# Branch B's output product by blocks of two with seven products, its operands and weight sums formed through HBM, and branch A's gate kept in HBM

## The chip, the cores and the metric

The kernel runs on one core of one Trainium2 chip. The metric is the device time of one execution in microseconds (us), the median of several runs. Names of engines: PE is TensorE (matmuls), DVE VectorE, ACT ScalarE, POOL GpSimd, SP SyncE, whose queue issues most DMAs.

## The reference

Two layers over 1024 latent tokens of width 1024. Layer 0 has two branches behind one input projection and one output projection; layer 1 is a pooling mixer and isn't touched by the change. Cut to layer 0:

```python
def layernorm(x, g, b):
    mu = jnp.mean(xf, axis=-1, keepdims=True)
    var = jnp.mean(jnp.square(xf - mu), axis=-1, keepdims=True)
    y = (xf - mu) * lax.rsqrt(var + LN_EPS) * g + b

def conformer_conv(va, vg, p):
    u = va * jax.nn.sigmoid(vg)
    u = depthwise_conv(u, p["conv_w"], p["conv_b"], CONV_PAD)     # 31 taps
    return jax.nn.silu(layernorm(u, p["ln_g"], p["ln_b"]))

def even_mixer(h, h0, p):
    z = h @ p["w_in"]
    va, vg, ga, xb, gb = jnp.split(z, [W_CONV, 2 * W_CONV, 3 * W_CONV, 3 * W_CONV + W_LRU], axis=-1)
    y_a = conformer_conv(va, vg, p) * jax.nn.silu(ga)
    y_b, hT = rglru_branch(xb, p, h0, True)      # short conv, gates, a scan in each direction
    y_b = y_b * jax.nn.silu(gb)
    return jnp.concatenate([y_a, y_b], axis=-1) @ p["w_out"], hT

# per layer: x = x + gate * even_mixer(modulate(rmsnorm(x), shift, scale)); shift, scale, gate = silu(c) @ mod_w + mod_b
```

## The kernel before

Activations stand transposed: eight tiles of 128 channels (rows) by 1024 tokens (columns), in two halves of 512 tokens, since one matmul writes 128 x 512. Every product is in three parts: an operand x is split into a rounded high part (a cast on ACT) and the rest (a subtraction, "low"), and hi·hi, hi·lo and lo·hi are added up in PSUM. A weight tile of 128 x 1024 comes as `wr` (raw, a ring of two buffers), is cast on ACT to `wh` and its low part `wl` formed on POOL (`raw_split`). A product over eight input tiles and both halves is 48 matmuls.

In the first layer the engines' orders are written out by hand: each call through `on(engine, ...)`, and its short forms `vec`, `act`, `cast` and `gp`, is tied behind the call before on that engine. So one late instruction holds all that stand behind it there. `fill(n)` puts n pieces of the depthwise convolution (DVE) between other work. The stages in order:

1. A loop over the eight channel tiles j: the products `va`, `vg`, `xb`, the recurrent branch's gates and its two scans on DVE. `rec_sum` adds the two directions (DVE, 128 x 1024) and SP stores the sum to `yb_raw[j]` in HBM. `at_rest` and the next block's weight loads follow.
2. The gate products `gb` of branch B with their SiLU (`gb_product`, `gb_silu`); `gated(n)` reloads `yb_raw[n]` through a ring of two buffers (`vtile`), multiplies and splits (ACT cast, POOL low).
3. The product with branch B's half of the output weights, `wob` (from the loop `for m in range(KT)` behind `wob_ps`): for each output tile m and half 24 matmuls, then `wob_evict`: ACT scales with the layer's gate into one of four buffers (`ttile`), SP loads x into a `vtile`, POOL adds, SP stores to `x1_part` in HBM. Under this product the rest of the convolution is done, and near its end the layer norm: `ln_mean`, then for each half `ln_square` and `ln_add` (DVE and ACT), `mean_parts` (cast `mh_ln` on ACT, low `ml_ln` on DVE), and `ms_ln`, two matmuls with a matrix of ones that sum over channels. `ln_root` (root on ACT, reciprocal on DVE), `ln_scale` (eight multiplications on DVE a half) and `ln_silu` (eight on ACT) follow.
4. The gate products `ga` of branch A (two of them in the fixed order), their SiLU and `ga_evict`, a multiplication on DVE out of PSUM. From here on (`fixed[0] = False`) a scheduler orders the work. Then branch A's half of the output product, `woa`, already by blocks of two with seven products (`quad`): with inputs and weights cut into 2 x 2 blocks, seven products of sums of blocks (`b11, t1, t2, b21, t3, b22, t4`) take the place of eight.
5. The second layer's modulation vector: `mod_halves` loads tiles of 128 x 512 into `ttile` buffers and multiplies them on DVE with the condition vector `cH`, with a running sum.

The gate's multiplications, means and tiles named here are the ones that the change moves.

Of the kernel before, what the change touches and what calls it, by code (L numbers as in the profile page):

```python
# [49 lines left out]

@with_exitstack
def body(ctx, tc, xT, ctxT, cc, ccol, modT, modW, win, gw, wout, wu, grp, wg, wo1, small, edge, ident, outT):
# [15 lines left out]
    y_raw = [{n: dram.tile([P, 2 * S], F32, tag=f"y_{n}_{p}", name=f"y_{n}_{p}") for n in BOPS} for p in range(2)]  # L68
    x1_part = [dram.tile([P, S], F32, tag=f"x1_part{j}", name=f"x1_part{j}") for j in range(KT)]
# [168 lines left out]
    a0 = base.tile([P, 2, KT], F32, name="a0")  # L238
    m1 = base.tile([P, 1, 3 * KT], F32, name="m1")
# [456 lines left out]
    def raw_load(src, name):  # L696
        raw = wpool.tile([P, D], F32, tag="wr", name=f"wr_{name}")
        nc.sync.dma_start(raw, src)
        return raw

# [76 lines left out]
    NSPREAD = 5  # L777

# [41 lines left out]
    with ExitStack() as actx:  # L820
# [56 lines left out]
        def rec_sum(st):  # L877
            hs, hb = st[2][1], st[2][3]
            vec(nc.vector.tensor_tensor, out=hs[:, C:], in0=hs[:, C:], in1=hb[:, C:], op=add)
            nc.sync.dma_start(yb_raw[st[0]], hs[:, C:])  # L880
# [22 lines left out]
        for j in range(KT):  # L903
# [73 lines left out]
            name = "gb1" if final else f"vg{j + 1}"  # L977
            raw = raw_load(win[4 * KT + 1] if final else win[KT + j + 1], name)
# [9 lines left out]
            if state is not None:  # L988
                for d in range(2):
                    rec_scan(state, d)  # L990
                rec_sum(state)
            at_rest()
            xb = wide(name if final else f"xb{j + 1}")
# [16 lines left out]
            fill(19 if state is None else 6)  # L1010
            state, uc = now, ucn


        gps = {0: [xb[:, h] for h in HALF]}
        gws = {}


        def gb_weights(j):
            src, name = ((win[4 * KT + j], f"gb{j}") if j < KT else
                         (wout[j - KT, 1], f"wob{j - KT}") if j < 2 * KT else  # L1020
                         (win[2 * KT + (0, KT // 2)[j - 2 * KT]], f"ga{(0, KT // 2)[j - 2 * KT]}"))
            gws[j] = raw_split(raw_load(src, name), name)

        def gb_product(j, w):
            if j == 4:
                gps[j] = (lambda t: [t[:, h] for h in HALF])(wide(f"gb{j}"))
            else:
                gps[j] = [psum(f"gb{j}_{h}") for h in range(2)]
            for h in range(2):
                all_of(mm3_fixed(gps[j][h], w, (hh, hl), HALF[h]))  # L1030
# [3 lines left out]
        def gb_silu(j):  # L1034
            sbs[j] = [ttile(f"sb{j}_{h}") for h in range(2)]
            for h in range(2):
                act(sbs[j][h], gps[j][h], AF.Silu)

        gb_product(1, w)
# [3 lines left out]
        gb_weights(2)  # L1043
        rec_exp(state)
        gb_product(2, gws[2])
# [3 lines left out]
        gb_weights(3)  # L1049
        gb_silu(0)  # L1050
        gb_silu(1)
        gb_product(3, gws[3])
        fill(24)
        rec_scan(state, 0)
        raw = raw_load(win[4 * KT + 4], "gb4")
        hi = wpool.tile([P, D], F32R, tag="wh", name="wh_gb4")
        lo = wpool.tile([P, D], F32R, tag="wl", name="wl_gb4")
# [4 lines left out]
        rec_sum(state)  # L1062
# [18 lines left out]

    KH = KT // 2
# [66 lines left out]
    def prod(ps, w, op, first, last):  # L1149
        xh, xl = op  # L1150
        for k in range(KH):
            hi, lo = w[:, k * P : (k + 1) * P], w[:, H + k * P : H + (k + 1) * P]
# [65 lines left out]
    bh, bl = [], []  # L1218
    def gated(n, between):
        th, tl = d2tile(f"ybh{n}", F32R), d2tile(f"ybl{n}", F32R)  # L1220
        for h in range(2):
            y = vtile(f"yr{n}_{h}")
            nc.sync.dma_start(y, yb_raw[n][:, HALF[h]])
            v = sbs[n][h]
            vec(nc.vector.tensor_tensor, out=v, in0=y, in1=v, op=mult)
            cast(th[:, HALF[h]], v)
            gp(out=tl[:, HALF[h]], in0=v, in1=th[:, HALF[h]].bitcast(F32), op=sub)
            fill(between)
        bh.append(th)
        bl.append(tl)  # L1230

    gb_product(4, gws[4])
    gated(0, 3)
    gb_silu(2)
    gb_weights(5)
    gb_product(5, gws[5])
    gated(1, 3)
    for j in range(3, KT + 1):
        if j == 4:
            gb_weights(j + 2)  # L1240
        if j < KT:
            gb_silu(j)
        if 4 < j < KT - 1:
            gb_weights(j + 2)
        if 3 < j < KT - 2:
            gb_product(j + 2, gws[j + 2])
        gated(j - 1, (0, 0, 4, 5, 5, 3, 1, 0)[j - 1])
        if j == KT:
            gb_weights(KT + 1)
            fill(8)  # L1250
        ln_sums()


    def wob_evict(m, h):
        v = ttile(f"wo_{m}_{h}")
        act(v, wob_ps[m][h], AF.Identity, scale=m0[:, 0, 2 * KT + m : 2 * KT + m + 1])
        t = vtile(f"xp{m}_{h}")
        nc.sync.dma_start(t, xT[m][:, HALF[h]])
        gp(out=t, in0=t, in1=v, op=add)
        nc.sync.dma_start(x1_part[m][:, HALF[h]], t)  # L1260


# [50 lines left out]
    wob_ps = {}  # L1313
    for m in range(KT):
        w = gws[KT + m]
        wob_ps[m] = [psum(f"wob{m}_{h}") for h in range(2)]
        steps = [mm3_fixed(wob_ps[m][h], w, (bh, bl), HALF[h]) for h in range(2)]
        if m == 0:
            for h in range(2):
                for _ in range(KT - 1):  # L1320
                    next(steps[h])
        for h in range(2):
            all_of(steps[h])
            if (m, h) == (KT - 2, 0):
                while ended[0] < KT:
                    fill(1)
                ln_sums()
                for q, parts in enumerate([mean_parts(lnacc[q][:, :H], f"mu{q}") for q in range(2)]):
                    ln_mean(q, parts)
            elif m >= KT - 2:  # L1330
                q = m - KT + 2
                for j in range(KT) if (m, h) != (KT - 1, 1) else ():
                    ln_square(j, q)
                    if j > 1:
                        ln_add(j - 2, q)
                if (m, h) != (KT - 1, 1):
                    for j in (KT - 2, KT - 1):
                        ln_add(j, q)
                    lnparts = mean_parts(lnacc[0][:, :H], "ln0") if q == 0 else lnparts
                else:  # L1340
                    ln_root(0, lnparts)
                    lnparts = mean_parts(lnacc[1][:, :H], "ln1")
            wob_evict(m, h)
            fill(7)
            ln_sums()
        gb_weights(KT + m + 2)


    gaps = {}

    def ga_product(j, w, h):
# [982 lines left out]
```

## Time and profile before

| | |
|---|---|
| runs: median of 3 (lowest to highest) | 1268.27 us (1267.44 to 1268.94) |
| the profiled execution: its span | 1263.6 us, 16209 instructions |
| busy in the span | PE 99%, DVE 90%, ACT 52%, POOL 23% |
| bytes moved | 182.29 MB, 144 GB/s in the mean |
| TensorE clock granted | full speed in all 40 slices |

A span is the time from the first to the last instruction that the profiler recorded; the profiled execution has no time of its own beside it, and the runs lie 4.7 us above that span. Busy times of matmuls overlap each other, so a stretch of matmuls is priced by the distance of their starts. In rows of a timeline the first number is the start in us, the second the time; a bracket says how long the engine idled before and what ended that. A row of a window has start and end, length, each engine's busy time with its count of instructions, the clock, the share of the DMA engines and GB/s.

### The profile page before, as it was taken

The page shows a single profiled execution, that of the slowest core. Times are in us where ns is not written, and L with a number is a line of the kernel's source. Part 1 is how long each engine was busy: PE and PEld are TensorE (multiplying, and loading weights), DVE is VectorE, ACT ScalarE, POOL GpSimd, SP SyncE. Part 2 cuts the span into 40 slices and gives each one's busy share as a digit, 9 for nine tenths or more (in the row PEclk, how much of TensorE's full clock was granted, in tenths as well). Part 3 has the DMA queues.
Part 4 walks back from the last instruction along what each step waited for, and adds up shares of the span by engine and source line. Part 5 has one row for each costly group of instructions (what it writes and reads, how often), then busy time and mean ns, then how long its engine had stood idle before and what let it go on. Part 6 is the DMA issues. An engine that isn't in the chain of part 4 may idle for free.

```text
span 1263.6 us, 16209 instructions
## 1 busy us (share of the span) xinstructions
PE 1249.8 (99%) x5866; PEld 1035.6 (82%) x5866; DVE 1139.3 (90%) x1746; ACT 653.8 (52%) x952; POOL 295.7 (23%) x176
## 2 busy tenths in 40 slices
PE   9999999999999999999999999999999999999997
PEld 7788888888888888888887878888888888888786
DVE  7799999999999999998978969999899987977975
ACT  8464566656666534237535445744343444644642
POOL 0015364436444547543210023000000000000002
PEclk9999999999999999999999999999999999999999
DMA  9970121112121233442436666344323334759723
GB/s 376 388 254 33 52 65 46 63 43 75 42 84 42 84 119 132 159 150 84 147 112 225 202 206 183 103 136 148 125 94 140 117 125 126 268 199 335 285 71 134
DMA packets 78705, 182.29 MB, mean 144 GB/s; under 512 B 7712, under 2 KB 23328, under 8 KB 78624
## 3 DMA queue, kind: packets, MB, share of 16 engines
q1 hardware_dynamic: 67328, 172.33, 39.8%
q10 hardware_dynamic: 11296, 8.92, 2.2%
q8 instruction: 46, 0.75, 0.2%
q14 instruction: 35, 0.29, 0.1%
HBM read 137.18 MB, written 44.04 MB: 143 GB/s over the span
## 4 chain that ended last, share of the span: by engine, by line
PE 70%; DVE 18%; DMA 7%; issue 2%; ACT 2%; POOL 1%; SPq 0%; POOLq 0%; ACTq 0%; DVEq 0%
PE wob L670 7%; DVE conv L670 5%; PE va L670 5%; PE xb L670 4%; PE vg L670 4%; DVE l L670 3%; PE fold L670 3%; PE g L670 3%; PE qb_v L1153 2%; PE ga L670 2%; PE qb_g L1156 2%; PE ga L161 2%; PE qb_v L1156 2%; PE qb_g L1155 2%; PE qb_g L1153 2%
## 5 line engine op out<-in xcount | busy, mean ns | idle before, releaser
L670 DVE SCALAR_TENSOR_TENSOR conv<-u,sm,conv 128x505 f32<-128x505 f32 (+6 forms) x224 | 153.6, 744 | 1.0
L2045 POOL TENSOR_TENSOR o<-x,rr 128x256 f32<-128x256 f32 (+1 forms) x10 | 9.2, 952 | 448.4 <-ACT rr L2045 448.4
L670 ACT ACTIVATE l<-g,sm 128x512 f32<-128x512 f32 (+1 forms) x96 | 58.7, 619 | 57.7 <-PE g L670 57.0
L670 POOL TENSOR_TENSOR l<-l,l 128x1280 f32<-128x1280 f32 x16 | 47.1, 2967 | 25.6 <-ACT l L670 15.1
L670 PE MATMUL gb<-h0h,wl_gb 128*128 128x512 f32 x128 | 49.9, 390 | 0.4 <-POOL wl_gb L670 0.4
L670 PE MATMUL va<-h0h,wl_va 128*128 128x512 f32 x128 | 49.9, 390 | 0.2 <-DVE wl_va L670 0.2
L98 ACT CAST wq_g<-wr_g 128x512 fp32r<-128x512 f32 x48 | 28.2, 621 | 41.9 <-DMA wr_g<-wg 15.6
L670 PE MATMUL gb<-h0l,wh_gb 128*128 128x512 f32 x128 | 49.8, 389 | 0.0
L670 PE MATMUL gb<-h0h,wh_gb 128*128 128x512 f32 x128 | 49.8, 389 | 0.0
L670 PE MATMUL va<-h0l,wh_va 128*128 128x512 f32 x128 | 49.8, 389 | 0.0
L670 PE MATMUL va<-h0h,wh_va 128*128 128x512 f32 x128 | 49.8, 389 | 0.0
L670 PE MATMUL wob<-ybl,wh_wob 128*128 128x512 f32 x128 | 49.8, 389 | 0.0
L670 PE MATMUL wob<-ybh,wl_wob 128*128 128x512 f32 x128 | 49.8, 389 | 0.0
L670 PE MATMUL wob<-ybh,wh_wob 128*128 128x512 f32 x128 | 49.8, 389 | 0.0
L670 DVE TENSOR_TENSOR_SCAN l<-l,l 128x256 f32<-128x256 f32 (+1 forms) x32 | 48.7, 1521 | 1.1
L670 DVE SCALAR_TENSOR_TENSOR conv<-cL,wsum,conv 128x506 f32<-128x506 f32 (+3 forms) x70 | 48.1, 745 | 0.2
L670 POOL TENSOR_TENSOR l<-l,uc 128x1280 f32<-128x1280 f32 x16 | 47.6, 2999 | 0.0
L98 ACT CAST wq_wo<-wr_wo 128x512 fp32r<-128x512 f32 x48 | 28.6, 620 | 35.5 <-DVE wr_wo L1134 12.4
L98 ACT CAST wq_v<-wr_v 128x512 fp32r<-128x512 f32 x48 | 28.1, 620 | 33.7 <-DMA wr_v<-wfold 16.6
L670 PE MATMUL xb<-h0l,wh_xb 128*128 128x512 f32 x112 | 43.8, 391 | 0.0
L670 PE MATMUL xb<-h0h,wh_xb 128*128 128x512 f32 x112 | 43.8, 391 | 0.0
L670 POOL TENSOR_TENSOR wl_xb<-wr_xb,wh_xb 128x1024 fp32r<-128x1024 f32 x7 | 16.8, 2407 | 114.5 <-ACT wh_xb L670 114.5
(680 smaller groups left out, 4362.5 us busy)
## 6 DMA issues: line engine op xcount, KB each, us to landing
modw<-modW SPq DMA_DIRECT2D x16, 512.0 KB, 10.2
mod<-modT SPq DMA_DIRECT2D x32, 256.0 KB, 3.4
wr_v<-wfold SPq DMA_DIRECT2D x16, 512.0 KB, 4.0
wr_g<-wg SPq DMA_DIRECT2D x16, 512.0 KB, 4.3
wr_wo<-wo SPq DMA_DIRECT2D x16, 512.0 KB, 4.1
mod<-modT SPq DMA_DIRECT2D x14, 512.0 KB, 4.5
y_b<-y SPq DMA_DIRECT2D x24, 256.0 KB, 3.5
y_t<-y SPq DMA_DIRECT2D x24, 256.0 KB, 3.1
```

Of the source, the lines that this page charges most:

```text
L98: return (nc.scalar.copy(hi, src), eng.tensor_tensor(out=lo, in0=src, in1=hi.bitcast(F32), op=sub))
L161: mm(ps, hi[:, kc], xh[k][:, cols], start=(k == 0), stop=False)
L670: last[eng] = f(*args, **kw)
L1153: nc.tensor.matmul(ps, hi, xh[k], start=(first and k == 0), stop=False, skip_group_check=not first)
L1155: nc.tensor.matmul(ps, hi, xl[k], start=False, stop=False, skip_group_check=not first)
L1156: mm = nc.tensor.matmul(ps, lo, xh[k], start=False, stop=(k == KH - 1), skip_group_check=not first)
L2045: tail[eng] = f(*args, **kw)
```

## The change

- **The product `wob`.** Its input and its weights are cut into 2 x 2 blocks as for `woa`: for each of four pairs of output tiles (q) seven products (k) of 12 matmuls (`prod_fixed`), in the order `b11, t1, t2, b21, t3, b22, t4`, into three banks a, c, b; after the first, ACT copies bank a to b. The products of the stage are counted o = 7q + k.
- **Its operands.** `gate(n)` leaves the gated branch B in an SBUF tile; `yb_sums` and `yb_last` form the sums of blocks (POOL and DVE), store each to HBM (`yb_op`), and `yb_load` / `yb_split` bring them back and split them.
- **Its weights.** The four block sums are formed in HBM in the block loop (`block_sum_steps`): SP copies 1 MB blocks, POOL's queue accumulates onto them by DMA. 14 of the pairs of blocks are loaded and split ahead, during the gate products, and both parts stored (`pair_ahead`); `pair` loads them again when they are due.
- **Branch A's gate.** All 16 gate products (`in_product(0)` to `in_product(15)`) come before `wob`. The SiLU of `ga` goes to HBM (`ga_evict` into `ga_raw`); `ga_gate` reloads it through the two `vtile` buffers and multiplies on DVE, 16 times.
- **Sums into HBM.** `x1_part` begins as a copy of x, and `wob_evict` adds to it by an accumulating DMA on POOL's queue; `rec_store` does so with the two directions of the scan, in place of `rec_sum`.
- **The order of the stage.** Layer norm, splits, gates and `mod` tiles are hung behind the products by `after(o, ...)`, all in the fixed order of the engines.

The core of the diff:

```diff
+        def rec_store(st, d):
+            latent = st[2][2 * d + 1][:, C:]
+            if d == 0:
+                nc.sync.dma_start(yb_raw[st[0]], latent)
+            else:
+                plus(yb_raw[st[0]], latent)
...
+    def pair_ahead(n):
+        raw = raw_pair(n)
+        hi, lo = d2tile(f"ph_{n}", F32R), d2tile(f"pl_{n}", F32R)
+        cast(hi, raw)
+        nc.sync.dma_start(wsplit[n][0], plain(hi))
+        low(gp, lo, raw, hi)
+        nc.sync.dma_start(wsplit[n][1], plain(lo))
...
+    def wob_evict(m, i, h, ps):
+        v = ttile(f"wo_{m}_{i}_{h}")
+        act(v, ps, AF.Identity, scale=out_gate(m, i))
+        plus(x1_part[m + i][:, HALF[h]], v)
...
+    def ga_gate(j, h):
+        v = vtile(f"ga_{j}_{h}")
+        nc.sync.dma_start(v, ga_raw[j][:, HALF[h]])
+        u = us[j][:, HALF[h]]
+        vtt(out=u, in0=u, in1=v, op=mult)
...
+        if n == 14:
+            for q in range(2):
+                ln_mean(q, lnparts[q])
+            squares(0)
+        if n == 15:
+            squares(1)
+            pair(0)
+            yb_load("t3", dtile)
+            pair(1)
+            yb_load("b22", dtile)
+            yb_load("t4", dtile)
...
+    after(0, yb_split, "t3", vtt)
+    after(2, yb_split, "b22", vtt)
+    after(3, yb_split, "t4", vtt)
+    after(0, parts_of, 0)
+    after(1, lambda: ln_root(0, lnparts[0]))
+    after(3, parts_of, 1)
+    after(4, lambda: ln_root(1, lnparts[1]))
+    after(4, ln_scale, 0)
+    for j in range(KT):
+        after(6, ln_silu, j, 0)
+    after(7, ln_scale, 1)
+    for j in range(KT):
+        after(9, ln_silu, j, 1)
+    for j in range(KT):
+        after(9 + j // 4, ga_gate, j, 0)
+        after(12 + j // 4, ga_gate, j, 1)
+    for n in range(2, 18):
+        after(max(1, 2 * n - 7), pair, n)
...
+    for o in range(7 * (KH - 1) - 7, 7 * (KH - 1)):
+        for _ in range((1, 2, 1, 2, 1, 2, 1)[o % 7]):
+            after(o, next, mods)
...
+    for q in range(KH):
+        m = 2 * q
+        a, c, b = psum(f"wob_a{m}"), psum(f"wob_c{m}"), psum(f"wob_b{m}")
+        for k, (ps, name, first, last_, out_) in enumerate((
+                (a, "b11", True, False, None), (c, "t1", True, False, (1, 1)), (b, "t2", False, False, (0, 1)),
+                (a, "b21", False, True, (0, 0)), (b, "t3", False, False, (1, 1)), (c, "b22", False, True, (0, 1)),
+                (b, "t4", False, True, (1, 0)))):
+            prod_fixed(ps, stream[7 * q + k], yb_operand(name), first, last_)
+            if k == 0:
+                cast(b, a)
+            if out_ is not None:
+                wob_evict(m, *out_, ps)
+            for f, args in late_steps.get(7 * q + k, ()):
+                f(*args)
```

Three places show what moved. The first is TensorE around the matmuls that sum the squares (`ms_ln`). Before, the last of the `wob` matmuls stand ahead of them:

```order
L670 MATMUL wob_1_4865<-ybh_4218,wl_wob_4744 128x512
L670 MATMUL wob_1_4865<-ybh_4232,wh_wob_4743 128x512
L670 MATMUL wob_1_4865<-ybl_4233,wh_wob_4743 128x512
L670 MATMUL wob_1_4865<-ybh_4232,wl_wob_4744 128x512
L670 MATMUL ms_ln_0_4950<-mh_ln_4848,ones_r 128x512
L670 MATMUL ms_ln_0_4950<-ml_ln_4849,ones_r 128x512
L670 MATMUL ga_0_4972<-h0h_538,wh_ga_4860 128x512
```

The same place after, on TensorE; `wob_c` and `wob_b` are two banks of the new product:

```order
L679 MATMUL wob_c_5164<-yb_t1l_4815,wh_pair_5131 128x512
L679 MATMUL wob_c_5164<-yb_t1h_4813,wl_pair_5132 128x512
L679 MATMUL ms_ln_0_5202<-mh_ln_5183,ones_r 128x512
L679 MATMUL ms_ln_0_5202<-ml_ln_5184,ones_r 128x512
L679 MATMUL wob_b_5165<-yb_t2h_4907,wh_pair_5141 128x512
L679 MATMUL wob_b_5165<-yb_t2l_4909,wh_pair_5141 128x512
```

The sums stood at the end of the `wob` product, behind all of it; now they stand behind the stage's second product, with 26 products of it still to come.

The second place is DVE's order around the operand of those sums (`ml_ln`, its low part; `lnsum` is the sum of squares of a half, `mu_4785` and `mu_5004` the means of the second half). Before:

```order
L670 TENSOR_TENSOR lnsum_901<-mu_1_4782,lsq_0_4843 128x512
L670 TENSOR_TENSOR ml_ln_4849<-lnsum_901,mh_ln_4848 128x512
L670 TENSOR_TENSOR u_1049<-u_1049,mu_4785 128x512
L670 TENSOR_TENSOR u_1400<-u_1400,mu_4785 128x512
L670 TENSOR_TENSOR u_1735<-u_1735,mu_4785 128x512
```

DVE after, from the end of the second half's squares on; `lnsum_953` is the first half's sum:

```order
L679 TENSOR_TENSOR mu_5004<-mu_5004,lsq_1_5122 128x512
L679 TENSOR_TENSOR lnsum_954<-mu_5004,lsq_1_5126 128x512
L679 TENSOR_TENSOR yb_t3l_5137<-yb_t3l_5137,yb_t3h_5135 128x1024
L679 TENSOR_TENSOR yb_t3l_5138<-yb_t3l_5138,yb_t3h_5136 128x1024
L679 TENSOR_TENSOR ml_ln_5184<-lnsum_953,mh_ln_5183 128x512
L679 TENSOR_TENSOR yb_b22l_5147<-yb_b22l_5147,yb_b22h_5145 128x1024
L679 TENSOR_TENSOR yb_b22l_5148<-yb_b22l_5148,yb_b22h_5146 128x1024
```

`ml_ln` of the first half was next to its sum; now the 15 instructions of the second half and two lows of the operand t3 stand between.

The third place is DVE's order at the end of the `ga_gate` multiplications (`u` the branch, `ga_1` the reloaded SiLU of the second half) and the `mod` tiles; before, these were ordered by the scheduler behind the fixed part. After:

```order
L679 TENSOR_TENSOR u_2815<-u_2815,ga_1_5511 128x512
L679 TENSOR_TENSOR u_3151<-u_3151,ga_1_5514 128x512
L679 TENSOR_TENSOR u_3485<-u_3485,ga_1_5517 128x512
L679 SCALAR_TENSOR_TENSOR mod_0_0_5542,m1p<-mod_0_0_5542,cH 128x512
L679 SCALAR_TENSOR_TENSOR mod_8_0_5545,m1p<-mod_8_0_5545,cH 128x512
L679 SCALAR_TENSOR_TENSOR mod_1_0_5567,m1p<-mod_1_0_5567,cH 128x512
```

The `mod` tiles come behind all sixteen gates; they are in the same four buffers as the evictions `wo` of the new product.

More of the change, by code (lines that the diff above doesn't have):

```diff
@@ L1254, in wob_evict, with low @@
[L1254 to L1260, printed above, removed]
+    plain = lambda t: t.bitcast(F32)
+    h0, h1 = HALF
+    R, T = [None] * KT, [None] * KH
+    def low(eng, out, src, hi):
+        eng(out=out, in0=src, in1=plain(hi), op=sub)
@@ new lines, in yb_last, with yb_load, yb_split @@
+    def yb_last(i):
+        q = R[KH + i]
+        vstt(q[:, h0], T[i][:, h1], q[:, h0])
+        yb_store("t4", i, q[:, h0])
+    yb = {}
+    def yb_load(name, alloc):
+        yb[name] = [[alloc(f"yb_{name}{v}{q}", F32R) for q in range(2)] for v in "hl"]
+        for q in range(2):
+            nc.sync.dma_start(plain(yb[name][1][q]), yb_op[name][:, q * S : (q + 1) * S])
+    def yb_split(name, eng):
+        for hi, lo in zip(*yb[name]):
+            cast(hi, plain(lo))
+            low(eng, lo, plain(lo), hi)
@@ new lines, in prod_fixed, with out_gate @@
+    def prod_fixed(ps, w, op, first, last):
+        (hi, lo), (xh, xl) = w, op
+        for k in range(KH):
+            kc = slice(k * P, (k + 1) * P)
+            for t, (a, b) in enumerate(((hi, xh), (hi, xl), (lo, xh))):
+                on("pe", nc.tensor.matmul, ps, a[:, kc], b[k], start=(first and k == 0 and t == 0),
+                   stop=(k == KH - 1 and t == 2), skip_group_check=not first)
+    def out_gate(m, i):
+        return gneg[:, m + 1 : m + 2] if i else m0[:, 0, 2 * KT + m : 2 * KT + m + 1]
@@ new lines, in body, with ya_rows, ya_split, ya_first @@
+    ya = {}
+    def ya_rows(name):
+        operand(ya, name, dtile if name in ("t2", "b21", "b22") else d2tile, "ya")
+        return ya[name]
+    def ya_split(name, src):
+        hi, lo = ya_rows(name)
+        for i in range(KH):
+            cast(hi[i], src(i))
+            low(vtt, lo[i], src(i), hi[i])
+    up = lambda h: lambda i: us[i][:, HALF[h]]
+    dn = lambda h: lambda i: us[KH + i][:, HALF[h]]
+    def ya_first():
+        ya_split("b11", up(0))
+        for i in range(KH):
+            gp(out=us[i][:, h0], in0=us[i][:, h0], in1=us[i][:, h1], op=sub)
@@ L1461, in body @@
+    fixed[0] = False
+    for name, src in (("t3", up(1)), ("b22", dn(1)), ("t4", dn(0))):
+        hi, lo = ya_rows(name)
+        for i in range(KH):
+            split(src(i), hi[i], lo[i], nc.vector)
+    pairs_ = [18]
+    def wo_weights(m):
+        n = 7 * (KH + m // 2)
+        while 2 * pairs_[0] < n + 7:
+            pair(pairs_[0])
+            pairs_[0] += 1
+        return tuple(stream[n + ORDER.index(k)] for k in range(1, 8))
+    w0 = wo_weights(0)
     x1 = [None] * KT
```

377 lines of the change are left out of this document (188 added, 189 removed).

## The prediction

> **What bounds the kernel now.** I read the page's busy times first, then the waits of TensorE, the groups of matmuls, the chain that ended last, and at last VectorE's timeline around the place where the change puts its work. The page says who is full, and TensorE's longest wait says whether that engine is ever kept waiting:
>
> ```profile
> span 1263.6 us, 16209 instructions
> PE 1249.8 (99%) x5866; PEld 1035.6 (82%) x5866; DVE 1139.3 (90%) x1746; ACT 653.8 (52%) x952; POOL 295.7 (23%) x176
> ...
> PE fin_ms L2045 <- DVE dg L2045: 1.2, 1, 1.2
> ```
>
> TensorE (PE) is busy in 99% of the span and never waits longer than 1.2 us, so the time is its work: fewer matmuls are a gain in full, and a wait that appears is a loss in full, as nothing behind it is idle to take it up. VectorE (DVE) at 90% is the engine with the least room. The span is 1263.6 us and the median of the runs 1268.27, 4.7 us more; I add each change of the span to the median. About 0.2% of it, 2.5 us, is what a measurement here can tell from nothing.
>
> The price of a matmul is not its duration, since matmuls overlap. The group of the removed product, then four steps of the chain:
>
> ```profile
> L670 PE MATMUL wob<-ybh,wh_wob 128*128 128x512 f32 x128 | 49.8, 389 | 0.0
> ...
> 119.20 10.88 PE vg L670 x48
> ...
> 490.61 70.72 PE wob L670 x312
> 561.33 0.92 PE mu L670 x4
> 562.25 16.33 PE wob L670 x72
> ```
>
> 389 ns is one matmul's time in the pipe; 48 in a row take 10.88 us, 312 take 70.72: 0.2267 us each. The old branch-B output product is 312 + 72 = 384 matmuls, 87.05 us.
>
> **What it removes.** Each block of two by two takes seven products of 12 matmuls instead of eight, and there are four: 4 x 7 x 12 = 336, 48 fewer. 48 x 0.2267 = **10.9 us less** on TensorE. The eight branch-A gate products (48 matmuls each) are only moved in front. VectorE loses eight additions of 1024 columns (`rec_sum`) in the block loop; TensorE waited for none of them, so that is worth nothing.
>
> **The first wait: the sums of the layer norm.** Now count time as t from the end of in_product(14), where the means are formed. The matmuls that sum the squares (`ms_ln_0`) stand behind in_product(15) and two of the new products: 0.9 + 10.88 + 2 x 2.72 = 17.2 us. On VectorE their operand `ml_ln` is now behind the squares of both halves and two low parts of the operand t3. What that takes, VectorE's timeline of before shows:
>
> ```profile
> 561.82 2.48 DVE L670 TENSOR_TENSOR u<-u,mu 128x512 f32<-128x512 f32 x4 [0.20 <-PE mu L670]
> ...
> 570.61 0.69 DVE L670 TENSOR_TENSOR lnsum<-mu,lsq 128x512 f32<-128x512 f32 x1
> 571.98 0.69 DVE L670 TENSOR_TENSOR ml_ln<-lnsum,mh_ln 128x512 fp32r<-128x512 f32 x1 [0.69 <-ACT mh_ln L670]
> ...
> 583.70 0.69 DVE L670 TENSOR_TENSOR lnsum<-mu,lsq 128x512 f32<-128x512 f32 x1
> 585.84 0.69 DVE L670 TENSOR_TENSOR ml_ln<-lnsum,mh_ln 128x512 fp32r<-128x512 f32 x1 [1.44 <-ACT mh_ln L670]
> 586.44 3.35 DVE L670 RECIPROCAL ms_ln<-sq_ln 128x512 f32<-128x512 f32 x1
> 589.83 4.87 DVE L670 TENSOR_TENSOR u<-u,ms_ln 128x512 f32<-128x512 f32 x8
> ...
> 598.61 4.87 DVE L670 TENSOR_TENSOR u<-u,ms_ln 128x512 f32<-128x512 f32 x8
> ...
> 436.55 1.20 DVE L670 TENSOR_TENSOR wl_gb<-wr_gb,wh_gb 128x1024 fp32r<-128x1024 f32 x1
> ```
>
> Both halves' squares run from 561.82 to 584.39, 22.6 us; with 0.9 for the means before, two lows of 1.20 and `ml_ln` of 0.69, the operand is there at t = 26.6, against 17.2. TensorE waits 9.4 us, up to 12 if the t3 casts on ScalarE, behind its own squares, come late. Before, the first half's `ml_ln` came right behind its own squares (571.98) and TensorE still had matmuls then. I take 10.
>
> **The second wait: gates, modulation tiles and the evictions.** From the means to the end of the scaling, VectorE took 561.82 to 603.48 before, 41.7 us. The six lows in between add 7.2: t = 50 or so. Then come 16 gate multiplications, each with a reload of 256 KB through two buffers. The nearest thing in the trace is the old gate of branch B, which reloads `yr` through the same two buffers; POOL's rows show its pace, and the DMA view the landings:
>
> ```profile
> 492.17 3.02 POOL L670 TENSOR_TENSOR ybl<-sb,ybh 128x512 fp32r<-128x512 f32 x2 [1.28 <-ACT ybh L670]
> 496.48 2.56 POOL L670 TENSOR_TENSOR ybl<-sb,ybh 128x512 fp32r<-128x512 f32 x2 [1.28 <-ACT ybh L670]
> ...
> yr<-yb_raw SPq DMA_DIRECT2D x16, 256.0 KB, 2.9
> mod<-modT SPq DMA_DIRECT2D x32, 256.0 KB, 3.4
> cH<-cc SPq DMA_DIRECT2D x2, 256.0 KB, 4.1
> ...
> 612.49 0.68 DVE L1386 SCALAR_TENSOR_TENSOR mod<-mod,cH 128x512 f32<-128x512 f32 x1
> ```
>
> Two loads every 4.3 us, so 16 gates take 34 us less the first pair, which is there early: 32. VectorE reaches the modulation products (`mod`) at t = 82. On ScalarE stand the evictions; of its rows before I use these, one eviction, one copy-like pass and eight SiLUs:
>
> ```profile
> 561.59 0.69 ACT L670 ACTIVATE wo<-wob,m 128x512 f32<-128x512 f32 x1 [2.95 <-PE mu L670]
> 562.54 0.60 ACT L670 ACTIVATE mu<-u 128x512 f32<-128x512 f32 x1 [0.26 <-DVE u L670]
> ...
> 593.18 5.75 ACT L670 ACTIVATE u<-u,sm 128x512 f32<-128x512 f32 x8
> ```
>
> The `mod` products stand in VectorE's fixed order, and they share a ring of four buffers (the t tiles) with the evictions of the new products. The eviction of product 16 of the stage (counted from 0, (b, t2) of the third block) takes the buffer of `mod1_1_0`, the third of these tiles, so it can't start before t = 82 + 3 x 0.68 + 0.7 = 85, and product 18 accumulates onto the same bank. With the first wait and some 1.5 us (an estimate) for the copy of product 7's bank, which product 9 needs and which stands near eight SiLUs of 5.75 us on ScalarE, TensorE would reach product 18 at 0.9 + 10.9 + 18 x 2.72 + 10 + 1.5 = 72: it waits 13 us. Then 16 `mod` tiles and four evictions go through four buffers: a landing of 3.4 and 0.68 for the multiplication make 4.1 per buffer, 1.0 per tile, 20.4 us; then the condition vector is loaded anew (`cH`, 4.1) with its SiLU (0.6), an eviction (0.7) and the copy that product 23 waits for (0.6). So product 23 starts at 82 + 26.4 = 108, where without any wait it would at 0.9 + 10.9 + 23 x 2.72 = 74. The stage loses 108 - 74 = **34 to 35 us**, both waits together; I take 35. If gates pace better (their 2.9 us landing by two buffers, 1.8 each with the multiplication) VectorE is at `mod` at 77 and the loss 30; if they queue behind the weight loads on SP, a few us more: 45. If TensorE is late for another reason, the chain stays: it starts with TensorE's own means.
>
> **The traffic ahead of it.** In SP's order lie 34.6 MB between the loads of the weights of products 7 and 13: split pairs stored and loaded, operands of branch B, copies of x and their loads. The rows of the stage before and of the busiest windows, the last two numbers being the DMA share and GB/s:
>
> ```profile
> 490.20:566.40 76.20, 76.20 (x337) 63.05 (x336) 71.33 (x106) 22.75 (x33) 41.41 (x25) 1.00 0.45 155
> ...
> 20.00:30.00 10.00, 10.00 (x58) 7.90 (x57) 8.44 (x11) 9.25 (x15) 0.00 (x0) 1.00 1.03 409
> ...
> 1100.00:1110.00 10.00, 10.00 (x46) 8.29 (x45) 8.30 (x11) 7.58 (x11) 0.00 (x0) 1.00 1.02 352
> ...
> 1160.00:1170.00 10.00, 10.00 (x46) 8.28 (x45) 7.38 (x11) 4.18 (x7) 0.00 (x0) 1.00 1.00 373
> ```
>
> The stage moved 155 GB/s; full engines moved 352 to 409. I estimate that SP is held at the first stores until about 463 (product 4 ends near 457.6, counted in steps of 10.88 back from 490.6; then a cast, a low of 2.4 and two POOL subtractions). The weights of product 13 must be on the chip near 541: 78 us. At 409 GB/s the bytes take 85 us, at 373 93 us, at 352 98 us: 7, 15 or 20 us late. The hold may be some us shorter, and SP runs ahead in the products after; at the lower end the loss is zero. I take **4**, nearest to the row with the highest rate. [...]
>
> **The block loop.** `rec_sum` becomes an accumulating DMA on POOL's queue, and six block sums of weights are accumulated there too, at one place three of 1 MB, ahead of the low part of `wl_vg`. No DMA on POOL's queue is in the trace before. The row of the instruction that stands behind them:
>
> ```profile
> 286.60 2.40 POOL L670 TENSOR_TENSOR wl_vg<-wr_vg,wh_vg 128x1024 fp32r<-128x1024 f32 x1 [14.36 <-DVE u L670]
> ```
>
> POOL had idled 14 us for VectorE there, so a queue that needs up to 3 us to issue changes nothing: 0 at best, a few us at each of two or three places at worst (10 in all). I take **1**. [...] Everything else (silu kept in HBM, evictions that add to `x1_part` by DMA instead of POOL's `xp` addition, the odd gates' sign) is off TensorE's path: nothing.
>
> **The sum:** -10.9 + 35 + 4 + 1 = +29, so 1268.3 + 29 = **1297 us**.
>
> **Rivals.** *Cover holds (13%).* TensorE never waits, as in the old kernel, and the saving comes out: 1268.3 - 10.9 = 1257, up to 1264 with a few small waits. It decides at two points: `ml_ln` must be there at t = 17 and VectorE must reach `mod` by t = 67. Against it speaks that the squares alone are 22.6 us; for it, that the old kernel hid its chain of 41.7 us, and that a reload could be twice as fast as I have it. *Only the first wait (5% that it nearly cancels, 16% that it is partly worse).* Gates done early, evictions not held: -10.9 + 10 to 12 = 1268 to 1270, no change; with a part of the second wait, 1271 to 1283. *The traffic decides (4%).* Weights late by 15 to 20 us and the accumulating DMAs slow: -10.9 + 35 + 20 + 10 = 1322. *The work isn't less:* excluded, as TensorE's program is 48 instructions shorter.
>
> **How the numbers follow.** My forecast, the whole chain, has 62%, from 1283 (a loss of 25 and 1 beside it) to 1318 (45, 10 and 5 in place of 35, 4 and 1). With the partial cases (16%) and the cancellation (5%) the range is 1266 to 1318, leaving out most of the 13% below and some 5% above. Faster by over 0.2% is the covered case: 0.13; within 0.2%: 0.05; slower: 0.62 + 0.16 + 0.04 = 0.82.
>
> **What the profile after would show.** Right: a wait of TensorE at `ms_ln_0` on VectorE's `ml_ln` of 9 to 12 us; VectorE idle before the `ga` multiplications on DMA, 2 us apiece; a wait at a product of the third block on ScalarE's eviction; PE busy near 1239 us in a longer span; the windows of the in products at 350 to 410 GB/s. Wrong: TensorE at 99%, no wait over 2 us; or waits of in products on their weights that are longer than those in the block stage.

## The result and the profile after

The changed kernel takes 1402.67 us (median of four runs, 1395.11 to 1409.5) against 1268.61 us for the kernel before (four runs, 1267.44 to 1269.89): the ratio is 1.1064, with a 95% interval of 1.1023 to 1.1105. That is 134 us slower, where 29 were forecast, within -2 to +50. The sign was right, and so was one mechanism; the size was not.

The page of the profile after, lines for the span, the engines, the slices of granted clock and DMA share, and POOL's DMA queue:

```profile
span 1402.2 us, 16501 instructions
PE 1276.8 (91%) x5818; PEld 1044.7 (75%) x5818; DVE 1156.4 (82%) x1700; ACT 667.4 (48%) x954; POOL 383.1 (27%) x229
...
PEclk9999999998999989888968899999999999999998
DMA  9961654632322799988976676624443333558823
...
q0 software_dynamic: 5760, 18.88, 7.8%
```

TensorE is no longer full, and in several of the slices 10 to 23 its granted clock has fallen as well. (Its busy time rose by 27 us though it has 48 matmuls less: slow matmuls count as busy, 0.63 us each behind the longest wait where they otherwise take 0.39.) The waits of TensorE, with total, times and longest:

```profile
PE wob_b L679 <- ACT wo L679: 39.4, 4, 25.0
PE in L679 <- ACT ga L679: 18.4, 3, 6.6
PE wob_b L679 <- ACT wob_b L679: 13.1, 2, 10.2
PE wob_c L679 <- ACT ga L679: 10.5, 1, 10.5
PE g L679 <- DVE u L679: 6.2, 1, 6.2
PE in L679 <- ACT yb L679: 6.1, 1, 6.1
```

The longest wait before was 1.2 us; now there are 39.4 us for evictions alone. Where they lie, the tile views of the matmuls say (first and last start):

```profile
L679 PE MATMUL gb<-h0h,wh_gb x16: 389/389/396, 412.9 to 429.7; 128*128 128x512 f32 x16
...
L679 PE MATMUL in<-h0h,wh_gb x16: 389/389/389, 430.4 to 440.6; 128*128 128x512 f32 x16
...
L679 PE MATMUL wob_a<-yb_b11h,wh_pair x16: 389/389/389, 636.1 to 744.3; 128*128 128x512 f32 x16
```

`gb` began at 396.0 before, so the block loop ends 16.9 us later. The 15 in products take 636.1 - 430.4 = 205.7 us, and their matmuls need 164.1 (15 x 10.88 and the means' 0.9). From 636.1 to the end of the last `woa` matmul's step (its start and 0.23 us) at 874.1 are 238.0 us; the new products need 336 x 0.2267 = 76.2, `ms_ln` 0.9 and `woa` took 78.0 before, 155.1 together. So the account of the profiled execution (1402.2 - 1263.6 = 138.6 us) is:

| part | us |
|---|---|
| first us of the kernel, ahead of the block loop | +1 |
| block loop | +16 |
| 15 in products | +42 |
| new products and `woa` | +83 |
| 48 matmuls fewer | -11 |
| second layer, scattered | +9 |

The rows add to 140; the parts' borders cost the rest. Taken across, the distances between matmul starts split the 141 us lost from the block loop to `woa` into 109 us of waits and 32 us beside them: some 25 of slow matmuls behind waits, the rest overlap that is lost at each wait.

### The profile page after: what moved, and what is told of

Same layout as the page of the kernel before. It is cut to its first block, busy times and chain, and to the rows that moved or that the text cites. A ratio compares the mean times of both kernels' runs of the same rounds, so it can differ in the third digit from the quotient of the medians.

```text
span 1402.2 us, 16501 instructions
## 1 busy us (share of the span) xinstructions
PE 1276.8 (91%) x5818; PEld 1044.7 (75%) x5818; DVE 1156.4 (82%) x1700; ACT 667.4 (48%) x954; POOL 383.1 (27%) x229
## 5 line engine op out<-in xcount | busy, mean ns | idle before, releaser
L679 PE MATMUL in<-h0h,wh_in 128*128 128x512 f32 x224 | 92.2, 412 | 24.5 <-ACT ga L679 18.4
L679 PE MATMUL in<-h0h,wl_in 128*128 128x512 f32 x224 | 91.7, 409 | 3.5 <-POOL wl_in L679 3.5
L679 PE MATMUL in<-h0l,wh_in 128*128 128x512 f32 x224 | 91.1, 407 | 0.0
L679 PEld LDWEIGHTS in<-h0h,wh_in 128*128 128x128 f32 x224 | 44.7, 200 | 35.7 <-ACT ga L679 20.1
L679 PEld LDWEIGHTS in<-h0h,wl_in 128*128 128x128 f32 x224 | 44.2, 197 | 16.2 <-POOL wl_in L679 6.9
L679 PEld LDWEIGHTS in<-h0l,wh_in 128*128 128x128 f32 x224 | 44.7, 199 | 9.4
L679 POOL DMA_DIRECT2D x_part<-wo x24 | 21.1, 904 | 106.9 <-ACT wo L679 106.8
L679 POOL TENSOR_TENSOR wl_in<-wr_in,wh_in 128x1024 fp32r<-128x1024 f32 x13 | 32.1, 2467 | 53.2 <-ACT wh_in L679 53.2
```

The lines of the kernel that those rows point to most:

```text
L679: last[eng] = f(*args, **kw)
```

## The experiments

Each is one edit of the changed kernel unless it says otherwise, and one profiled execution. The stages are the three of the account; the kernel before took 1263.8 to 1267.8 us beside them. Where a kernel's edit doesn't touch a stage, the 15 in products took 202 to 210 us and the new products with `woa` 235 to 239, so less than 4 us is not read as an effect. The changed kernel's own four executions span 14 us, so a single time is read only together with its stages: those of e6, e7, e8 and e11 lie inside that span.

| kernel | first `gb` | in products | new products, `woa` | time |
|---|---|---|---|---|
| changed kernel | 412.9 | 205.7 | 238.0 | 1402.7 |
| e1 no block sums | 396.4 | 207.5 | 236.8 | 1383.1 |
| e2 sum on DVE | 396.4 | 202.2 | 238.9 | 1383.0 |
| e3 four pairs ahead | 414.1 | 180.6 | 240.5 | 1378.9 |
| e4 mods late | 411.9 | 209.0 | 216.4 | 1383.2 |
| e5 no gate reload | 412.8 | 204.5 | 220.9 | 1381.0 |
| e6 evict early | 412.4 | 208.2 | 243.0 | 1409.4 |
| e7 subtractions on DVE | 412.5 | 208.9 | 238.4 | 1404.2 |
| e8 copies of x early | 413.1 | 205.6 | 238.9 | 1402.1 |
| e9 no split stores | 412.7 | 191.9 | 235.4 | 1381.5 |
| e10 gate buffers | 412.8 | 205.1 | 231.2 | 1394.3 |
| e11 wait filled | 411.9 | 209.7 | 235.8 | 1399.7 |
| e12 pairs in place | 413.1 | 196.1 | 237.6 | 1390.0 |
| e13 e4 and e5 | 412.1 | 206.9 | 206.4 | 1369.4 |
| e14 in place, no stores | 411.9 | 172.3 | 237.2 | 1362.7 |
| c1 four mended | 396.5 | 176.5 | 225.7 | 1345.7 |
| c3 six mended | 397.0 | 186.4 | 217.2 | 1343.7 |

### The block loop: e1 and e2

Edits: e1 drops the call `block_sum_steps(j)` and lets `op_source` read plain blocks; e2 puts `rec_sum` back:

```diff
-                    rec_store(state, d)
+                rec_sum(state)
```

> The block sums of the weights are left out (neither copies nor accumulating DMAs; the products read plain blocks instead, so their result is another). In the changed kernel the block loop ends 16.9 us later than before (first gb matmul 412.93 against 396.03), with one VectorE instruction of 8 columns taking 11.56 us beside an unbroken stretch of POOL work that begins with two DMA commands. Theory A, the block sums' commands push POOL's work together and VectorE's instruction is held until POOL pauses: without them gb begins at 397 to 400 and the span falls by 13 to 16 us. Rival B, it is the other commands (the accumulation of yb_raw) or the shifted order of the convolution pieces: gb still begins at 410 to 413. The stages behind it should take what they took (205 us for the 15 in products, 238 us from the first new product to the last woa matmul), within 5 us.

> Only the sum of the two scan directions goes back to VectorE (rec_sum, 8 additions of 1.23 us, stored by SP); the block sums stay on POOL's queue. Theory A (block sums' commands): the hold of VectorE stays, gb begins at 408 to 414. Rival B (the accumulation of yb_raw, or the place where the 8-column instruction falls): it goes, gb begins at 397 to 401. In the in products nothing changes: 205 us, within 5.

Either edit alone ends the stall (`gb` at 396.4 in both): e1 as theory A has it, e2 as rival B has it. (Both times fell by 20 us, more than this stall; the rest lies in later stages, within their scatter.) So neither theory holds as written: the block sums alone are not the cause, nor is the accumulation of `yb_raw`; what both edits change is when a small VectorE instruction meets POOL. In the changed kernel, POOL's timeline (start, length), then VectorE's:

```profile
287.72 0.90 POOL L679 DMA_DIRECT2D yb_raw<-l  x1 [9.26 <-DVE l L679]
288.33 1.17 POOL L679 DMA_DIRECT2D wsum<-wsum  x1
288.89 3.00 POOL L679 TENSOR_TENSOR wl_vg<-wr_vg,wh_vg 128x1024 fp32r<-128x1024 f32 x1
291.23 6.46 POOL L679 TENSOR_TENSOR l<-l,uc 128x1280 f32<-128x1280 f32 x2
297.05 3.00 POOL L679 TENSOR_TENSOR wl_va<-wr_va,wh_va 128x1024 fp32r<-128x1024 f32 x1
```

```profile
288.52 11.56 DVE L679 SCALAR_TENSOR_TENSOR edge_junk<-u,sm 128x8 f32<-128x8 f32 x1
```

An instruction of eight columns, both of whose inputs are in SBUF, took 11.56 us: it ended at 300.08, as POOL's last row of this stretch did (300.05). In e2 the same instruction, and behind it POOL's first:

```profile
286.13 0.16 DVE L679 SCALAR_TENSOR_TENSOR edge_junk<-u,sm 128x8 f32<-128x8 f32 x1
```

```profile
286.99 2.41 POOL L679 TENSOR_TENSOR wl_vg<-wr_vg,wh_vg 128x1024 fp32r<-128x1024 f32 x1 [13.58 <-issue]
```

There it is done in 0.16 us, 0.9 us ahead of POOL's stretch. In the changed kernel it came 0.8 us behind the first DMA command of that stretch. Everything late in that block follows from it: `uc` on VectorE, its cast on ScalarE, the `xb` weights and TensorE's waits of 2.4 and 6.2 us.

### The in products: e3, e8, e9, e12, e14

The edits, in this order: `NSPLIT`, the place of the copies, the stores, the tile in which the pair is split; e14 is e9 and e12 together.

```diff
-NSPLIT = 14
+NSPLIT = 4
...
     def block_sum_steps(j):
+        with held(latest[0]):
+            nc.sync.dma_start(x1_part[j], xT[j])
...
+        if n == 0:
             nc.sync.dma_start(wsplit[n][0], plain(hi))
...
-        raw = raw_pair(n)
         hi, lo = d2tile(f"ph_{n}", F32R), d2tile(f"pl_{n}", F32R)
+        raw = plain(lo)
+        for i in range(2):
+            latest[0] = nc.sync.dma_start(raw[:, HALF[i]], op_source(2 * n + i))
         cast(hi, raw)
```

> Four instead of 14 weight pairs are split ahead and stored; the other ten are loaded raw and split when they are due. That takes 15 MB (10 times a load of 0.5 MB and two stores of 0.5 MB) out of the 56 MB that the in products' 205 us carry, and 5 MB out of the stage behind. Theory D, the DMA engines are the bound there (share 0.90 to 0.94 at 317 to 334 GB/s): 41 MB at 330 GB/s are 124 us, less than TensorE's 164, so the 15 in products take 165 to 175 us and the waits on wr_in go. Rival O, it is SP's order (a store that waits for its split holds the weight loads behind it): a loss of 20 us or more stays, 185 us and above. The stage of the new products may lose 0 to 10 us by ten more casts and lows on ScalarE and POOL, or gain as much by 5 MB less.

Ten pairs less take 25 us out of the stage. What is left is a wait of 6.6 us at `in_product(8)` and a few around the means. 180.6 lies between the two expectations, 6 us above theory D's and 4 below rival O's, and the edit takes turns of the raw buffers away with the bytes, so it settles neither.

> The eight copies of x into x1_part (0.5 MB each, HBM to HBM) are issued in the block loop, where the DMA engines carry 62 to 130 GB/s, instead of among the in products. Theory D (the engines are the bound in the in products): 4 MB less of 56, at 320 GB/s 12 us less: 193 us instead of 205.7 for the 15 in products, perhaps less as a copy reads and writes HBM. Rival O (SP's order): 203 to 207. The block loop should not change by more than 3 us, unless the hold of VectorE falls at another place.

4 MB less changed nothing: 205.6, as rival O (SP's order) has it. Bytes alone are not the cause, and theory D in its plain form fell.

> Of the 14 split pairs only the first is stored; the other 26 stores of 0.5 MB are left out (all 14 are loaded from the first pair's place, so the result is another). Loads, casts and lows and the two raw buffers stay as they are. Moving the copies of x away (4 MB) had changed nothing, splitting ten pairs less ahead (15 MB, and ten turns of the raw buffers less) took 25 of 41 us. Theory D (bytes ahead of the weight loads, so that a load lands in 5 to 9 us instead of 3.5): 13 MB less let the loads land in 4 us and the 15 in products take 170 to 185 us. Theory R (two raw buffers, three turns per product, each a load, a cast and a low): a turn is the load's 3.5 to 5 us, 1.05 and 2.4 to 2.5; three turns through two buffers are 11 to 13 us against TensorE's 10.88 even with free engines, so 190 to 200 us.

191.9, 14 us less: inside R's range and 7 above D's. So the stores count, and they are not all.

> The pairs split ahead are loaded into the tile of their low part and split there, so they no longer pass through the two raw buffers; every byte, cast, low and store stays. Theory R (the two raw buffers, three turns a product): the 13 weight loads have the buffers to themselves, the waits on wr_in fall to what a late landing leaves, and the 15 in products take 170 to 185 us instead of 205.7. Theory D (the engines' load alone, loads that land in 5 to 9 us): 195 to 206.

196.1, 10 us less: in D's range, and far from R's 170 to 185. But this is not D unchanged, for with the raw buffers out of the way the DMA engines became full; a window of the changed kernel, then of e12 (the last two numbers are DMA share and GB/s):

```profile
512.00:545.00 33.00, 24.94 (x96) 19.63 (x96) 21.42 (x34) 7.92 (x12) 15.79 (x8) 0.86 0.92 330
```

```profile
512.00:598.00 86.00, 71.23 (x270) 55.90 (x269) 69.91 (x101) 19.54 (x25) 41.06 (x19) 0.87 0.99 362
```

> Pairs split in place as in e12, and only the first one stored (the result is another). If raw buffers and stores are two separate causes (R and D), the 15 in products take 165 to 172 us, TensorE's own 164 and the wait at the ninth product. If one of them was the whole cause, the time is that of e12 or of e9 (191.9) within 4 us.

172.3, at the upper edge of what was expected of two causes, against TensorE's 164.1: of 41.6 us lost 33.4 are gone, while the edits alone took 14 and 10. Two limits, the raw buffers and the stores, stood behind each other, and taking one away only showed the other. The window of e14, where TensorE is nearly full again at a share of 0.83:

```profile
512.00:598.00 86.00, 80.73 (x345) 65.06 (x344) 77.41 (x114) 28.78 (x39) 56.82 (x24) 0.98 0.83 277
```

How the two meet is seen on ScalarE in the changed kernel, whose cast of the weights waits for the load, with a buffer that POOL's low of a pair had to free first:

```profile
529.77 1.05 ACT L679 CAST ph<-wr_pair 128x1024 fp32r<-128x1024 f32 x1 [8.07 <-DMA wr_pair<-wsum]
533.14 1.05 ACT L679 CAST ph<-wr_pair 128x1024 fp32r<-128x1024 f32 x1 [2.31 <-DVE conv L679]
543.53 1.04 ACT L679 CAST wh_in<-wr_in 128x1024 fp32r<-128x1024 f32 x1 [9.34 <-DMA wr_in<-win]
```

Behind that cast stood the SiLU that frees the bank of the product before last; so the page says that TensorE waits for "ACT ga", where the load was late.

Why the stores cost is not taken apart. Leaving them out takes away 13 MB, and with them the places where SP holds every later load behind a store whose cast or low isn't done. SP's own waits of the changed kernel from 430 to 640 (total, times, longest), at the stores of the high and of the low parts:

```profile
SPq L1323 <- ACT ph L679: 14.1, 6, 3.9
SPq L1325 <- POOL pl L679: 6.3, 5, 2.3
```

In e12 the engines were full (0.99), which speaks for the bytes there. In the changed kernel, at 0.92, SP's order (rival O) is not excluded.

### The new products: e4, e5, e13, e10

Edits: `next(mods)` ten times behind `w0 = wo_weights(0)` in place of `after(o, next, mods)` (e4); an empty `ga_gate` (e5); both (e13); the t tiles for two gates of four (e10):

```diff
-        v = vtile(f"ga_{j}_{h}")
+        v = (vtile if j % 4 % 3 == 0 else ttile)(f"ga_{j}_{h}")
```

> The mod tiles are taken out of the fixed order of products 14 to 20 and left to the scheduler behind the fixed part. Theory M, as predicted: the evictions of products 16 to 20 wait for buffers that mod tiles hold behind the 16 gate reloads. Without them the waits of 25.0, 10.2 and 9.8 us of wob_b on ScalarE's evictions and copy go, and the time from the first new product to the last woa matmul (238.0 us) falls by 35 to 55. Rival G, the gate reloads themselves are the bound, as branch A's operands need them: the wait moves to the first woa products, and the fall is under 20 us.

> The 16 gate reloads and their multiplications on VectorE are left out (branch A isn't gated, so the result is another). In the changed kernel they take from 681.3 to 727.9 us, 46.6 us, and the mod tiles that evictions wait for stand behind them. Theory M, the gates' reloads hold the mod tiles and these the evictions: the mod tiles begin some 45 us earlier, the 25.0 us wait of wob_b goes whole, and 238.0 us from the first new product to the last woa matmul fall by 25 to 35; the waits of about 10 us at products 23 and 27 stay, as they come from the second load of the condition vector and from the sums for branch A. Rival: the mod tiles alone, 16 through four buffers, hold the evictions too: the wait only shrinks, fall under 15 us.

> Mod tiles out of the fixed order and the gate reloads left out as well (branch A isn't gated, the result is another). Alone they took 22 and 17 us from the 238.0 us of the new products and woa. If they are one chain, reloads first and the mod tiles behind them, so that either still holds the evictions or branch A's operands: together 40 to 50. If they are the same wait: 22 to 28. What is left above 155 us then belongs to the squares, the copies between banks and the late operands of branch A.

> Half of the gate reloads go into the four t buffers, so that up to four loads can be under way instead of two. Theory M (two buffers pace the reloads, 46.6 us for 16): they take 25 to 32 us, the wait at product 18 shrinks from 25 to 5 to 12 us, and the stage of 238.0 us falls by 10 to 20. Rival (the loads are late behind the pair loads in SP's order, or evictions and reloads now wait for each other in the t buffers): no fall, or longer.

Alone they take 22 and 17 us, together 32: less than their sum of 39, more than either, and in neither range that was expected of e13 (40 to 50, or 22 to 28): partly one wait, partly two. In e4 the wait of 25 us is gone, but branch A's first product now waits 7.7 us for its operand and the last new product still waits 10.0: between the expectations M and G. In e5 the wait at product 18 is 7.6 us, not gone: again between the two expectations. In e10 the reloads took 37 us instead of 47, the wait 13.5 instead of 25, and the stage 7 us less: theory M's direction in all three, and short of its range in all three. The chain itself stands as it was predicted, in VectorE's and ScalarE's rows of the changed kernel:

```profile
681.28 1.29 DVE L679 TENSOR_TENSOR u<-u,ga 128x512 f32<-128x512 f32 x2
691.51 0.69 DVE L679 TENSOR_TENSOR u<-u,ga 128x512 f32<-128x512 f32 x1 [8.94 <-DMA ga<-ga_raw]
...
727.30 0.69 DVE L679 TENSOR_TENSOR u<-u,ga 128x512 f32<-128x512 f32 x1 [1.74 <-DMA ga<-ga_raw]
727.91 0.68 DVE L679 SCALAR_TENSOR_TENSOR mod<-mod,cH 128x512 f32<-128x512 f32 x1
```

```profile
703.38 0.69 ACT L679 ACTIVATE wo<-wob_c,gneg 128x512 f32<-128x512 f32 x1 [4.61 <-DMA x_part<-wo]
730.00 0.69 ACT L679 ACTIVATE wo<-wob_b,m 128x512 f32<-128x512 f32 x1 [25.93 <-DVE mod L679]
```

16 gates end at 728, 46.6 us after the first; the `mod` tiles follow at once; behind the third of them ScalarE's eviction starts, which had waited 25.93 us, and behind that product 18 at 730.74.

### The edges of the stage: e6 and e7

e6 calls `ga_evict(n)` and `parts_of(0)` ahead of `squares(1)`; e7 turns two `gp` into `vtt`:

```diff
+            ga_evict(n)
+            parts_of(0)
             squares(1)
...
-            gp(out=us[i][:, h0], in0=us[i][:, h0], in1=us[i][:, h1], op=sub)
+            vtt(out=us[i][:, h0], in0=us[i][:, h0], in1=us[i][:, h1], op=sub)
```

> The SiLU of the last in product (which frees the bank that product 1 needs) and the first half's parts of the squares' sum are put ahead of the second half's squares on ScalarE and VectorE. Theory S, the squares of both halves ahead of it are the 10.5 us wait of wob_c: that wait goes, to 2 us or less, and with the clock's 2 us behind it the stage starts 10 to 12 us earlier. As the layer norm's chain isn't shorter by it (the squares end when they did), the wait at product 18 grows by about as much, and the sum of the stage (238.0 us) falls by 0 to 5 us only. Rival: the waits are independent, the stage falls by 10 to 12.

The 10.5 us wait went, and waits of 5.5 (`ms_ln`) and 10.4 us (the copy of bank a) came: the stage took 243.0. Theory S says rightly that nothing is gained, but the wait at product 18, which it expected to grow, stayed (24.0), and that the stage grew by 5 is not explained further.

> The eight subtractions that form branch A's sums t1 and t3 go from POOL to VectorE. In the changed kernel four lows of 0.68 us take VectorE 13.12 us there, beside an unbroken stretch of POOL work from 763.6 to 779.4. Theory A (VectorE with two operands in SBUF is held until POOL pauses): the lows take 3 us, the eight subtractions 5.4 more, and the 9.8 us wait of wob_b at the last new product goes: 238.0 falls by 8 to 12. Rival: the wait comes from SP's loads or the evictions' DMAs: it stays, fall 0 to 3.

The last new matmul came 147.4 us into the stage instead of 157.0, and the 9.8 us wait halved, as theory A has it. But the stage took 238.4: the time came back in `woa`, which waited for evictions and weights. VectorE's four lows in the changed kernel, then POOL's low of a weight pair and VectorE's last row of its stretch in e7:

```profile
767.47 13.12 DVE L679 TENSOR_TENSOR ya_t1l<-u,ya_t1h 128x512 fp32r<-128x512 f32 x4
```

```profile
772.68 19.20 POOL L679 TENSOR_TENSOR wl_pair<-wr_pair,wh_pair 128x1024 fp32r<-128x1024 f32 x1
787.18 2.50 DVE L107 TENSOR_TENSOR ya_t4l<-u,ya_t4h 128x512 fp32r<-128x512 f32 x4
```

The hold was turned round: with the subtractions on VectorE its stretch was unbroken from 765.5 to 789.7, and now one instruction of POOL, 2.4 to 3.0 us long elsewhere, took 19.20 and ended 2.2 us behind that stretch. A `woa` product waited 2.0 us for its result. So the hold was real and moving it was no gain.

### A filled wait: e11

```diff
+            if (q, k) == (2, 4):
+                for _ in range(9):
+                    prod_fixed(idle, stream[7 * q + k], yb_operand(name), True, True)
             prod_fixed(ps, stream[7 * q + k], yb_operand(name), first, last_)
```

> Nine products (108 matmuls, 24.5 us) of the same operands into a bank that nothing reads are added ahead of product 18, where TensorE waits 25 us; the result stays. Theory C (after an idle wait of more than some 2 us the first matmuls run at half pace for about 4 us, at a cost of about 2 us each time): product 18 begins when it did, 94 to 96 us after the stage's first matmul, and its matmuls are 0.227 us apart at once: the stage of 238.0 us falls by 1 to 3 us in spite of 108 more matmuls. Rival (the slow pace has another cause, such as DMA traffic or operands): it stays, and the stage keeps its time or grows.

Product 18 began 94.5 us into the stage (94.7 without the filling), and the stage was 2.2 us shorter with 108 matmuls more; that is inside the scatter, but 24.5 us of work would not be. TensorE's rows at its start, first of the changed kernel, then of e11:

```profile
730.74 0.79 PE L679 MATMUL wob_b<-yb_t3h,wh_pair 128*128 128x512 f32 x1 [25.02 <-ACT wo L679]
731.33 0.63 PE L679 MATMUL wob_b<-yb_t3l,wh_pair 128*128 128x512 f32 x1
731.75 0.63 PE L679 MATMUL wob_b<-yb_t3h,wl_pair 128*128 128x512 f32 x1
...
734.32 0.40 PE L679 MATMUL wob_b<-yb_t3h,wl_pair 128*128 128x512 f32 x1
734.55 0.40 PE L679 MATMUL wob_b<-yb_t3h,wh_pair 128*128 128x512 f32 x1
```

```profile
733.58 0.50 PE L679 MATMUL wob_b<-yb_t3h,wh_pair 128*128 128x512 f32 x1 [1.17 <-ACT wo L679]
733.92 0.40 PE L679 MATMUL wob_b<-yb_t3l,wh_pair 128*128 128x512 f32 x1
734.16 0.39 PE L679 MATMUL wob_b<-yb_t3h,wl_pair 128*128 128x512 f32 x1
```

After 25 us of idling the starts are 0.43 us apart until 734.3; with the wait filled they are 0.23 apart at once. So idling is the cause of the slow pace, not traffic nor operands.

### Edits together: c1 and c3

c1 is e2, e3, e4 and e7; c3 is e2, e4, e7, e8, e10 and e12.

> Four edits together: rec_sum on VectorE, four pairs split ahead, mod tiles left to the scheduler, sums for branch A on VectorE. If the terms add up: block loop 16, in products 25, stage of the new products 22 and about 2 for the rest of the matmuls' pace, from 1402.7 to about 1335 to 1345. If one wait hides behind another (the gates' reloads keep branch A's operands late): 1345 to 1360.

> Six edits together: rec_sum on VectorE, pairs split in place, copies of x in the block loop, mod tiles left to the scheduler, half of the gate reloads through the t buffers, sums for branch A on VectorE. If the terms add up: 16, 25 to 35, 22 and 7 to 15 less, 1402.7 to between 1315 and 1335. If the waits of the new products' stage hide each other: 1335 to 1350. In no case does it come below the kernel before.

1345.7 and 1343.7: 57 and 59 us of the 134 come back, and the terms hide each other as the second halves of both expectations say (c1's 1345.7 lies at the border of both). Both stay 6% above the kernel before. No version of the experiments beat it.

## Why the prediction was wrong

**The removed work** was right: 48 matmuls, 10.9 us.

**The first wait** (10 us) had the right cause and the wrong door. `ms_ln` itself waited 0.3 us at first. The eviction of the last `ga` product stands behind the second half's squares on ScalarE, and product 1 needs its bank: 10.5 us, by the same squares. I had followed the new order on VectorE and TensorE, and not the bank through ScalarE's.

**The second wait** was the right mechanism at the right place, too small by half at product 18: "it waits 13 us" was 25.0. VectorE reached the reloads 7 or 8 us later than forecast, and they paced at 2.9 us each instead of 2.0, 46.6 us in all instead of 32. I had taken their pace and their landing of 2.9 us from a stage that moved 155 GB/s; during the reloads the changed kernel moved 253, and its DMA view gives this:

```profile
ga<-ga_raw SPq DMA_DIRECT2D x16, 256.0 KB, 4.9
```

With two buffers and 0.69 for the multiplication that makes an estimated 2.8 us each. The wait was also not the last: behind product 23 I had nothing, where waits of 3.3 and 9.8 us followed, and more in `woa`. The part lost 83 us, where I had 35: about 59 up to product 23, as far as the forecast's 35 went, and 24 behind it.

**The traffic** is the step that failed most: "I take 4, nearest to the row with the highest rate". The in products lost 42. Two things were wrong. The rate: with loads and stores mixed, the engines at a share of 0.92 moved 330 GB/s, below even the lowest full row that I had shown, 352, and far from the 409 on which I set the term; e12's full window has 362 at a share of 0.99. What sets the rate no run here shows. And the bytes were not the whole cost: three turns a product through two raw buffers were the second limit, shown by e12 and e14. Whether the stores cost by their bytes or by SP's order stays open.

**The block loop** ("I take 1") cost 16, and not in the queue where I looked for it: a small VectorE instruction met POOL's unbroken stretch. The prediction put the loss of `rec_sum` at nothing; e2, which puts it back, ends the stall. The "up to 3 us to issue" was my estimate, which no row of before showed; in the changed kernel a command took POOL 0.9 to 1.2 us and the three of the block sums in a row 2.9 (241.9 to 244.8), and 256 KB on POOL's queue landed in 5.5 us in the median (`x_part<-wo`, DMA view). The 16 came from the hold. I had named rows of POOL that idled; what mattered was who else would run beside them once they were moved.

**A term was missing**: what a wait costs behind itself. Some 25 of the 141 us lost are matmuls at half pace after waits, and 32 with the overlap lost at each wait. Neither the sum nor the bounds had it; TensorE's busy time, forecast near 1239 us, was 1276.8.

**The range** was too narrow because the terms were. Its upper end had 45, 10 and 5 us in them; the worst values that the prediction names, 45, 20 and 10, would have made it 1332, still 70 us short.

Left open: why e6 lost 5 us more, the 9 us scattered over the second layer, and what would take away the 51 us that e13 still loses in the new products and `woa` (206.4 us against 155.1). 42 of them are waits, the longest 11.4 us at product 27 for an eviction, 10.0 at product 1 behind the squares, and 8.4 in `woa` for an eviction; no run took all three away.

## What to carry to other kernels

A kernel in which one engine is 99% busy, as this one, pays for every wait in full, so a change that saves 11 us of its work has to be judged by the chains that it puts in front of it: follow each moved step through all engines' fixed orders, with banks and buffers as links of the chain. Price a transfer by the rate and landing time of the stage after the change, not of the stage before, and count turns of a ring (load, cast, subtraction) beside bytes. When one limit is taken away and little is gained, take the second away as well before either is acquitted (14 and 10 us alone, 33 together).

## What the runs showed of the hardware

**A wait of TensorE costs more than its length.** Over the changed kernel, e5, e9, e10, e12 to e14, c1 and c3, from 320 to 860 us, behind waits up to 1.7 us the next matmuls nearly always lost 0.1 to 0.4 us, unless another wait had just gone before or followed. Between 1.8 and 3.2 us it varied from 0.1 to about 3: behind 2.89 us the changed kernel lost 1.7 (679.4) and e5 0.1 (678.3). Behind waits of 3.3 us and more they ran 0.43 us apart instead of 0.2267 for 2.7 to 6.7 us, a loss of 1.4 to 3.4 (waits less than 1.5 us apart counted as one). In the changed kernel the clock granted in such a stretch was 0.50 (730.7 to 734.3, behind the wait of 25.02 us, 1.8 lost) and 0.52 (649.4 to 652.5, behind 10.49, 1.5 lost).

**VectorE can be held far longer than one POOL instruction.** 11.56 us for eight columns, beside six POOL instructions one behind the other: VectorE got no turn until POOL's stretch was over, and in e7 POOL's instruction none until VectorE's was (19.20 us). Beside POOL's two lows from 842.16 to 847.38 of the changed kernel `mod<-mod,cH`, with both inputs in SBUF, took 2.23 us (0.69 elsewhere), while `x<-qb_woa,m,x`, with one of them in PSUM, took its usual 0.74. It isn't always a hold to the end: from 763.6 to 770.4 the two took turns, VectorE's lows at 1.8 us each (0.68 elsewhere) and POOL's subtractions at 1.7. What decides between the two no run here shows. Another place for the instruction was worth the whole hold (e1 and e2, 16 us).
